# An encoder layer in float32: seven block products instead of eight for one request's MLP, and a pass of its own for the other's

## The chip, the cores and the metric

The kernel runs on one core of a Trainium2 chip. The metric is the device time of one execution in microseconds. Three executions of the kernel before took 2460.19 to 2464.03 us, with a median of 2462.54 us.

## The reference, cut to what matters

One layer of a bidirectional encoder runs on two requests with shared weights: the prompt (512 tokens of 1024 numbers) and the sample (1024 tokens). The change touches the last step, the MLP with a squared ReLU, with 4096 hidden columns.

```python
D_MODEL = 1024
BATCH = 1
SEQ = 512
...
DEC_BATCH = 1
DEC_SEQ = 1024
...
D_FF = 4 * D_MODEL
...
def squared_relu_mlp(x, w_up, w_down):
    return jnp.square(jax.nn.relu(x @ w_up)) @ w_down

def encoder_trunk(x, mem, ln_in_g, ln_in_b, w_in, rpb, g_mix_a, g_mix_b, w_out, ln1_g, ln1_b,
                  w_xq, w_xkv, w_xo, ln2_g, ln2_b, w_up, w_down, ln3_g, ln3_b):
    x = layer_norm(x, ln_in_g, ln_in_b)
    for l in range(DEPTH):
        x = layer_norm(ALPHA * x + token_mixer(x, w_in[l], rpb[l], g_mix_a[l], g_mix_b[l], w_out[l]),
                       ln1_g[l], ln1_b[l])
        x = layer_norm(ALPHA * x + memory_cross_attention(x, mem, w_xq[l], w_xkv[l], w_xo[l]),
                       ln2_g[l], ln2_b[l])
        x = layer_norm(ALPHA * x + squared_relu_mlp(x, w_up[l], w_down[l]), ln3_g[l], ln3_b[l])
    return x
...
def reference(x_prompt, x_sample, mem_prompt, mem_sample, ln_in_g, ln_in_b, w_in, rpb, g_mix_a,
              g_mix_b, w_out, ln1_g, ln1_b, w_xq, w_xkv, w_xo, ln2_g, ln2_b, w_up, w_down,
              ln3_g, ln3_b):
    y_prompt = encoder_trunk(x_prompt, mem_prompt, ln_in_g, ln_in_b, w_in, rpb, g_mix_a, g_mix_b,
                             w_out, ln1_g, ln1_b, w_xq, w_xkv, w_xo, ln2_g, ln2_b, w_up, w_down,
                             ln3_g, ln3_b)
    y_sample = encoder_trunk(x_sample, mem_sample, ln_in_g, ln_in_b, w_in, rpb, g_mix_a, g_mix_b,
                             w_out, ln1_g, ln1_b, w_xq, w_xkv, w_xo, ln2_g, ln2_b, w_up, w_down,
                             ln3_g, ln3_b)
    return (y_prompt, y_sample)
```

## The kernel before

All matrix products are made in three passes to keep float32's accuracy. An operand x is split into a high part (a copy rounded to float32r by ScalarE) and a low part (x minus the high part, by GpSimd or VectorE). `mm3` then sums high*high, high*low and low*high in PSUM, so 128 x 128 stationary and 128 x 512 moving columns cost three matmuls (L127 to L129).

The tokens lie in three groups of 512: group 0 is the prompt, groups 1 and 2 are the halves of the sample. Phase 0 makes the memory's keys and values, phase 1 the two attention mixtures, phase 2 the output projection, the cross-attention and the second layer norm. `ln2` (from L803) normalises a tile of 128 tokens, transposes it on TensorE and splits the result into high and low parts (L137 and L138); `X2[g]` holds the two parts of the transposed group.

Phase 3, from L851, is the MLP. The outer loop (L900) runs over 32 blocks f of 128 hidden columns. Per f, `col_block` loads 128 columns of `w_up` in two pieces of 256 KB, and `down_weights` loads 128 rows of `w_down` in two more; a piece goes through one of two `wraw` buffers, is copied by ScalarE (L104, L882) and subtracted by GpSimd (L105, L883). The buffer is free again when GpSimd is done. For each of the three groups, `up` makes 24 matmuls into a bank `pj`, then ScalarE applies the ReLU (L871), VectorE squares (L872), ScalarE copies the high part (L874) and GpSimd makes the low part (L875). `down` makes 24 matmuls, three to a bank of `t` or `s` for each of four token tiles and two halves of the columns, and VectorE adds every bank to the sums in `toks` (L897). So one pair of weight blocks serves 144 matmuls: 72 up and 72 down.

The last three blocks are handled apart (`LAST`, from L906): their hidden columns are kept, so that one tile of tokens after the other is finished, normalised by `layer_norm` (L147 on) and stored while TensorE still works on the next.

What stands in program order is not what runs in order: a scheduler of the framework orders each engine's instructions ahead of time by its own estimate. At run time each engine takes its list strictly in that order, and the DMAs all stand in one list, SyncE's. SBUF is cut into fixed slots: `tok` 8, `qt`, `pt`, `gb`, `kv` 2 each of 1024 columns, `cpr` 2 and `q` 7 of 512 and 528, six big `act` tiles, and in `wp` three `wh`, three `wl` and the two `wraw`.

## Time and profile before

| | us |
|---|---|
| median of three executions | 2462.54 |
| lowest and highest | 2460.19, 2464.03 |
| the profiled execution, from the first to the last instruction (span) | 2464.6 |
| TensorE busy in it | 2391.0 |
| VectorE, ScalarE, GpSimd busy | 1468.6, 858.5, 867.0 |

The profiled execution's own time is known by its span; it lies 2.1 us, or 0.1%, above the median. Busy times are sums over all stages. TensorE's matmuls overlap in the pipeline (one takes 390 ns from start to end while the next starts far earlier), so the number of matmuls that start in a stretch says more than the time of one.

### The profile page before, as it was taken

The numbers are of one execution on the slowest core, as the hardware profiler recorded it, in microseconds if no ns is written. First come the engines' busy times: TensorE is split into PE (matmuls) and PEld (weight loads), VectorE is DVE, ScalarE is ACT, GpSimd is POOL, SyncE is SP. The second block draws the span as 40 slices with busy tenths as digits, with TensorE's granted clock in tenths as the row PEclk, the third lists the DMA queues.
The fourth block names the chain that finished last, engine by engine and source line by source line (L and its number), as shares of the span: only waits on it lengthen the run. The fifth ranks groups of instructions, "written<-read, shape, count | busy, mean of one in ns | idle before, by whom it ended". The sixth has DMA issues, their size and how long they took to land.

```text
span 2464.6 us, 32262 instructions
## 1 busy us (share of the span) xinstructions
PE 2391.0 (97%) x11512; PEld 1983.0 (80%) x11512; DVE 1468.6 (60%) x3054; ACT 858.5 (35%) x1887; POOL 867.0 (35%) x790
## 2 busy tenths in 40 slices
PE   8989999999999999999999999999999999999997
PEld 6868778888888778778778788888888888888886
DVE  6256546666666785666666755555555555555538
ACT  4346645555555534333233211111111111111122
POOL 7555442221243135332353332222222223323346
PEclk9999999999999999999999999999999999999999
DMA  9665345554344543335323301111101011111112
GB/s 322 200 191 163 83 126 136 125 119 108 75 117 121 162 132 121 120 121 169 103 94 117 106 26 34 35 35 35 33 28 35 26 35 35 30 31 35 35 35 103
DMA packets 254641, 231.45 MB, mean 94 GB/s; under 512 B 65680, under 2 KB 196752, under 8 KB 254480
## 3 DMA queue, kind: packets, MB, share of 16 engines
q1 hardware_dynamic: 254480, 229.39, 32.2%
q8 instruction: 91, 1.49, 0.3%
q14 instruction: 70, 0.57, 0.1%
HBM read 170.16 MB, written 34.10 MB: 83 GB/s over the span
## 4 chain that ended last, share of the span: by engine, by line
PE 80%; DVE 6%; DMA 2%; ACT 2%; issue 1%; POOL 1%; SPq 0%; DVEq 0%; POOLq 0%; ACTq 0%
PE pj L127 15%; PE pj L128 15%; PE pj L129 15%; PE s L127 4%; PE s L129 4%; PE s L128 4%; PE t L127 3%; PE t L128 3%; PE t L129 3%; PE o L489 3%; PE t L473 2%; PE s L447 2%; PE s L448 1%; DVE tok L158 1%; PE t L499 1%
## 5 line engine op out<-in xcount | busy, mean ns | idle before, releaser
L105 POOL TENSOR_TENSOR wl<-wraw,wh 128x512 fp32r<-128x512 f32 x144 | 192.5, 1354 | 371.1 <-ACT wh L104 304.3
L897 DVE TENSOR_TENSOR tok<-tok,s 128x512 f32<-128x512 f32 x232 | 158.3, 685 | 234.5 <-PE s L129 234.3
L104 ACT ACTIVATE wh<-wraw 128x512 fp32r<-128x512 f32 x144 | 84.7, 625 | 305.5 <-PE pj L128 197.5
L431 ACT ACTIVATE q<-q,st 128x256 f32<-128x256 f32 (+3 forms) x256 | 138.3, 545 | 75.3 <-DVE st L430 72.5
L897 DVE TENSOR_TENSOR tok<-tok,t 128x512 f32<-128x512 f32 x232 | 152.0, 683 | 9.8 <-PE t L129 9.2
L477 DVE TENSOR_TENSOR pt<-t,pt 128x512 fp32r<-128x512 f32 x160 | 105.4, 671 | 85.6 <-ACT pt L476 85.1
L883 POOL TENSOR_TENSOR wl<-wraw,wh 128x512 fp32r<-128x512 f32 x64 | 84.0, 1330 | 185.3 <-ACT wh L882 180.9
L295 POOL TENSOR_TENSOR wl<-wraw,wh 128x256 fp32r<-128x256 f32 x128 | 94.4, 761 | 150.8 <-ACT wh L294 137.1
L871 ACT ACTIVATE cpr<-pj 128x512 f32<-128x512 f32 x96 | 56.9, 592 | 253.2 <-PE pj L129 251.7
L872 DVE TENSOR_TENSOR cpr<-cpr 128x512 f32<-128x512 f32 x96 | 93.1, 970 | 78.9 <-ACT cpr L871 78.8
L875 POOL TENSOR_TENSOR qt<-cpr,qt 128x512 fp32r<-128x512 f32 x45 | 61.5, 1366 | 190.1 <-ACT qt L874 146.5
L476 ACT ACTIVATE pt<-t 128x512 fp32r<-128x512 f32 x160 | 89.5, 583 | 88.5 <-PE o L489 85.0
L875 POOL TENSOR_TENSOR pt<-cpr,pt 128x512 fp32r<-128x512 f32 x46 | 64.7, 1407 | 156.6 <-ACT pt L874 149.3
L489 PE MATMUL o<-pt,tok 128*128 128x256 f32 (+3 forms) x560 | 113.5, 313 | 5.7 <-ACT q L495 4.1
L117 POOL TENSOR_TENSOR wl<-wraw,wh 128x512 fp32r<-128x512 f32 x48 | 63.2, 1333 | 126.1 <-ACT wh L116 120.6
L127 PE MATMUL pj<-x20h,wh 128*128 128x512 f32 x256 | 100.0, 391 | 0.1
L127 PE MATMUL pj<-x22h,wh 128*128 128x512 f32 x256 | 99.9, 390 | 0.0
L127 PE MATMUL pj<-x21h,wh 128*128 128x512 f32 x256 | 99.8, 390 | 0.0
L128 PE MATMUL pj<-x20l,wh 128*128 128x512 f32 x256 | 99.8, 390 | 0.0
L128 PE MATMUL pj<-x21l,wh 128*128 128x512 f32 x256 | 99.8, 390 | 0.0
L129 PE MATMUL pj<-x21h,wl 128*128 128x512 f32 x256 | 99.8, 390 | 0.0
L128 PE MATMUL pj<-x22l,wh 128*128 128x512 f32 x256 | 99.8, 390 | 0.0
(381 smaller groups left out, 7216.9 us busy)
## 6 DMA issues: line engine op xcount, KB each, us to landing
wraw<-in_w_in_dram SPq DMA_DIRECT2D x96, 256.0 KB
wraw<-in_w_up_dram SPq DMA_DIRECT2D x64, 256.0 KB
wraw<-in_w_down_dram SPq DMA_DIRECT2D x64, 256.0 KB
kv<-in_c_rope_dram SPq DMA_DIRECT2D x24, 512.0 KB
hd<-qt SPq DMA_DIRECT2D x96, 128.0 KB
wraw<-in_w_out_dram SPq DMA_DIRECT2D x48, 256.0 KB
wraw<-in_w_xq_dram SPq DMA_DIRECT2D x48, 256.0 KB
wraw<-in_w_xo_dram SPq DMA_DIRECT2D x48, 256.0 KB
```

The source lines that it names most:

```text
L105: G.tensor_sub(wl[:, sl], r, f32(wh[:, sl]))
L127: T.matmul(out, lh[k], rh[k], start=(k == 0), stop=False, skip_group_check=True)
L128: T.matmul(out, lh[k], rl[k], start=False, stop=False, skip_group_check=True)
L129: T.matmul(out, ll[k], rh[k], start=False, stop=(k == n - 1), skip_group_check=True)
L295: G.tensor_sub(dl, src, f32(dh))
L431: A.activation(p, p, AF.Exp, bias=nm, accum_out=den)
L476: A.activation(hi[:, 0:x], t[:, 0:x], AF.Copy)
L477: V.tensor_sub(lo[:, 0:x], t[:, 0:x], f32(hi[:, 0:x]))
L489: T.matmul(o[:, q0:q0 + n], v(c, h), part[:, x:x + n], start=(done == 0 and part is hi), stop=(done == total - 1 and part is lo), skip_gro ...
L872: V.tensor_mul(a, a, a)
L875: G.tensor_sub(hl, a, f32(hh))
L897: V.tensor_add(x, x, q)
```

## The change

The sample's 1024 tokens are no longer run as two groups with eight block products per projection. Each of its two MLP matrix products is seen as a product of 2 x 2 blocks: the left operand (tokens, or hidden columns) in two halves of the rows and two of the inner dimension, the weights likewise. Seven block products are formed from sums and differences of blocks and combined into the four output blocks by additions. `PRODUCTS` lists for each of the seven which left blocks and which weight blocks are added or subtracted, and into which output blocks the result goes, with its sign; five of the seven need a sum on the left, five a sum of weights, and five go into two output blocks, two into one.

- `ln2` keeps the sample's transposed tokens in float32 (one tile per half; no split), and writes all normalised tokens to DRAM (`x2s`).
- The prompt's MLP is a loop of its own: per f the same four weight pieces now serve 24 up and 24 down matmuls. The hidden low part is made by VectorE.
- In its rounds 3 to 9, `left` forms the seven left operands of the sample's up projection: VectorE adds (five of seven), ScalarE copies the high part, VectorE makes the low part in a `kv` slot, and a DMA of 512 KB stores it in DRAM (`sa`): 28 tiles.
- The sample's up projection: for each of the seven products the left operand is loaded again (2 MB), and for each of 16 blocks f one or two weight pieces of 256 KB are loaded into `q` slots, added by VectorE if two, copied by ScalarE and subtracted by GpSimd (`right`); 12 matmuls follow into one bank, and the bank is copied (ScalarE) or added (VectorE) to the hidden columns, which stay in SBUF in float32. A finished hidden block is squared by VectorE.
- The sample's down projection: for each product 16 steps c. VectorE forms the left sum (five of seven products), ScalarE and VectorE split it, VectorE forms the weight sum (five of seven) and its low part; 12 matmuls go into four banks that hold the sums of all 16 steps. Then the four banks are added to one or two blocks of the output. GpSimd has no part in this.
- `finish` normalises and stores a half of the sample: the first half behind the sixth product, so beside the seventh, the second half at the very end.

The core of the diff:

```diff
-    x2s = dr.tile([512, D], F32, name="x2s")
+    x2s = dr.tile([1536, D], F32, name="x2s")
+    sa = [dr.tile([4, P, 2, 512], F32, name=f"sa{i}") for i in range(7)]
...
-            X2.append(new_act(f"x2{gi}"))
+            X2.append(new_act("x20") if gi == 0 else act.tile([P, 8, 512], F32, name=f"xt{gi}", tag="act"))
             GB[gi] = [[bcast(d[n][0], "gb")] for n in ("ln2_g", "ln2_b")]
-        layer_norm(toks[gi][t], *GB[gi])
+        x = toks[gi][t]
+        layer_norm(x, *GB[gi])
+        S.dma_start(x2s[(4 * gi + t) * P:(4 * gi + t + 1) * P], x)
         if gi == 0:
-            S.dma_start(x2s[t * P:(t + 1) * P], toks[gi][t])
-        split_t(toks[gi][t], *X2[gi], t * P)
+            split_t(x, *X2[0], t * P)
+            return
+        for kk in range(2):
+            o = bank("t").rearrange("p (j c) -> p j c", j=4)
+            for j in range(4):
+                T.transpose(o[:, j, :], x[:, (4 * kk + j) * P:(4 * kk + j + 1) * P], ident)
+            A.activation(X2[gi][:, 4 * kk:4 * kk + 4, t * P:(t + 1) * P], o, AF.Copy)
...
+    PRODUCTS = {
+        1: (((0, 0), ADD, (1, 1)), ((0, 0), ADD, (1, 1)), (((0, 0), ADD), ((1, 1), ADD))),
+        2: (((1, 0), ADD, (1, 1)), ((0, 0),), (((1, 0), ADD), ((1, 1), SUB))),
...
+    UP, DOWN = (5, 3, 2, 4, 1, 7, 6), (3, 5, 4, 2, 7, 1, 6)
...
+    def left(i):
+        blk = lambda b, k: X2[1 + b[0]][:, 4 * b[1] + k]
+        what = PRODUCTS[i][0]
+        for k in range(4):
+            x = blk(what[0], k)
+            if len(what) > 1:
+                y = slot("cpr")
+                V.tensor_tensor(y, x, blk(what[2], k), op=what[1])
+                x = y
+            t = slot("kv", dt=F32R)
+            A.activation(t[:, 0:512], x, AF.Copy)
+            V.tensor_sub(t[:, 512:1024], x, f32(t[:, 0:512]))
+            S.dma_start(sa[i - 1][k], f32(t).rearrange("p (j c) -> p j c", j=2))
...
-    toks[0] = [slot(tag) for tag in ("kv", "kv", "gb", "gb")]
+    toks[0] = [slot("tok") for _ in range(4)]
...
-        hh, hl = dst or parts(("pt", "qt")[next(turn) % 2])
+        hh, hl = slot("q", 512, F32R), slot("q", 512, F32R)
...
-        G.tensor_sub(hl, a, f32(hh))
+        V.tensor_sub(hl, a, f32(hh))
...
-    LAST = 3
-    for f in range(32 - LAST):
+    def down(h, w, first):
+        for t in range(4):
+            tt = slice(t * P, (t + 1) * P)
...
+    for f in range(32):
         w, dn = col_block(wup, f * P), down_weights(f)
-        for g in range(3):
-            h = up(g, w)
+        down(up(w), dn, f == 0)
+        if 3 <= f < 10:
+            left(UP[f - 3])
+    gb3 = [[bcast(d[n][0], "gb")] for n in ("ln3_g", "ln3_b")]
+    for t in range(4):
+        layer_norm(toks[0][t], *gb3, 1)
+        S.dma_start(outs[0][0, t * P:(t + 1) * P], toks[0][t])
...
+    def hidden(b, f):
+        if b not in H:
+            H[b] = ([slot("tok") for _ in range(8)] if b == (1, 0) else
+                    [act.tile([P, 8, 512], F32, name=f"h{b[0]}{b[1]}", tag="act") for _ in range(2)])
+        if b == (1, 0):
+            return H[b][f // 2][:, f % 2 * 512:f % 2 * 512 + 512]
+        return H[b][f // 8][:, f % 8]
...
+    def square(b, f):
+        x = hidden(b, f)
+        V.scalar_tensor_tensor(x, x, 0.0, x, op0=ALU.max, op1=ALU.mult)
...
+    def right(what, load, low, tag=None):
...
+        x = load(what[0])
+        if len(what) > 1:
+            z = load(what[2])
+            y = slot("cpr")
+            V.tensor_tensor(y, x, z, op=what[1])
+            x = y
+        t = wp.tile([P, 1024], F32R, name="wh", tag=tag or ("wh", "wl")[next(ring) % 2])
+        A.activation(t[:, 0:512], x, AF.Copy)
+        low.tensor_sub(t[:, 512:1024], x, f32(t[:, 0:512]))
+        return t[:, 0:512], t[:, 512:1024]
...
+    done = set()
+    lefts = {0: left_load(0), 1: left_load(1)}
+    for n, i in enumerate(UP):
+        _, what, into = PRODUCTS[i]
+        xs_ = lefts.pop(n)
+        for f in range(16):
+            if f == 8 and 0 < n < 6:
+                lefts[n + 1] = left_load(n + 1)
+            wh_, wl_ = (x.rearrange("p (k c) -> p k c", k=4) for x in right(what, up_block(f), G))
+            o = bank(("pj", "s", "t")[f % 3])
+            mm3(o, [wh_[:, k] for k in range(4)], [wl_[:, k] for k in range(4)],
+                [xs_[k][:, 0] for k in range(4)], [xs_[k][:, 1] for k in range(4)])
+            for b, op in into:
+                h = hidden(b, f)
+                if (b, f) not in done:
+                    done.add((b, f))
+                    A.activation(h, o, AF.Copy, scale=1.0 if op == ADD else -1.0)
+                else:
+                    V.tensor_tensor(h, h, o, op=op)
+            b = {2: (0, 1), 7: (1, 0), 6: (0, 0)}.get(i)
+            if b is not None:
+                square(b, f)
...
+    def finish(h):
+        for t in range(4):
+            layer_norm(accs[h][t], [g3[:, 0], g3[:, 1]], [g3[:, 2], g3[:, 3]], 1 if t % 2 else 2)
+            row = 512 * h + t * P
+            S.dma_start(outs[1][0, row:row + P], accs[h][t])
...
+    for n, i in enumerate(DOWN):
+        lw, rw, into = PRODUCTS[i]
+        banks = [bank(tag) for tag in (("pj", "pj", "s", "s") if n % 2 == 0 else ("t", "t", "t", "o"))]
+        for c in range(16):
+            x = hidden(lw[0], c)
+            if len(lw) > 1:
+                y = wp.tile([P, 512], F32, name="wraw", tag="wraw", bufs=2)
+                V.tensor_tensor(y, x, hidden(lw[2], c), op=lw[1])
+                x = y
+            a = wp.tile([P, 1024], F32R, name="wh", tag="wh")
+            A.activation(a[:, 0:512], x, AF.Copy)
+            V.tensor_sub(a[:, 512:1024], x, f32(a[:, 0:512]))
+            rh, rl = right(rw, down_block(c), V, "wl")
             for t in range(4):
-                down(g, t, [h], [dn], first=(f == 0))
-    # the last blocks' hidden columns are kept, so that a tile of tokens is finished at once
-    hs = [[None] * LAST for _ in range(3)]
-    ws = [col_block(wup, f * P) for f in range(32 - LAST, 32)]
-    for g in range(3):
-        hs[g][0] = up(g, ws[0])
-    hs[0][1] = up(0, ws[1])
-    hs[0][2] = up(0, ws[2], (slot("q", 512, F32R), slot("q", 512, F32R)))
-    keep = [act.tile([P, 8, 512], F32R, name="keep", tag="act") for _ in range(2)]
-    for i in (1, 2):
-        for g in (1, 2):
-            n = 4 * (i - 1) + 2 * (g - 1)
-            hs[g][i] = up(g, ws[i], (keep[0][:, n], keep[1][:, n]))
-    dn = [down_weights(f) for f in range(32 - LAST, 32)]
-    for g in range(3):
+                lh, ll = a[:, t * P:(t + 1) * P], a[:, 512 + t * P:512 + (t + 1) * P]
+                T.matmul(banks[t], lh, rh, start=(c == 0), stop=False)
+                T.matmul(banks[t], lh, rl, start=False, stop=False)
+                T.matmul(banks[t], ll, rh, start=False, stop=(c == 15))
+            if n == 0:
+                square((1, 1), c)
         for t in range(4):
-            down(g, t, hs[g], dn)
-            layer_norm(toks[g][t], g3, b3, 2 if g == 2 and t >= 2 else 1)
-            n = 4 * g + t
-            dst = outs[0][0, n * P:(n + 1) * P] if g == 0 else outs[1][0, (n - 4) * P:(n - 3) * P]
-            S.dma_start(dst, toks[g][t])
+            for b, op in into:
+                x = accs[b[0]][t][:, b[1] * 512:(b[1] + 1) * 512]
+                if (b, t) not in done:
+                    done.add((b, t))
+                    V.scalar_tensor_tensor(x, x, ALPHA, banks[t], op0=ALU.mult, op1=op)
+                else:
+                    V.tensor_tensor(x, x, banks[t], op=op)
+        if i == 7:
+            g3 = act.tile([P, 8, 512], F32, name="g3", tag="act")
+            for j, name in enumerate(("ln3_g", "ln3_b")):
+                src = d[name][0]
+                S.dma_start(g3[:, 2 * j:2 * j + 2].rearrange("p a c -> p (a c)"),
+                            bass.AP(tensor=src.tensor, offset=src.offset, ap=[[0, P], [1, D]]))
+        if i == 1:
+            finish(0)
+    finish(1)
```

Three places in the engines' lists. The first is SyncE's list in the MLP. Before, a round of the loop is four weight pieces and nothing else (`wraw` is the buffer, the source is the weight):

```order
L90 DMA wraw_17253<-in_w_down_dram 128x512
L90 DMA wraw_17472<-in_w_up_dram 128x4x128
L90 DMA wraw_17476<-in_w_up_dram 128x4x128
L90 DMA wraw_17482<-in_w_down_dram 128x512
L90 DMA wraw_17486<-in_w_down_dram 128x512
```

With the change, in the prompt's rounds 3 to 9 (L91 is the weight load, L888 the store of a left operand's tile from a `kv` slot):

```order
L91 DMA wraw_14586<-in_w_up_dram 128x4x128
L888 DMA sa2_66<-kv_14452 128x1024
L91 DMA wraw_14592<-in_w_down_dram 128x512
L888 DMA sa2_66<-kv_14456 128x1024
L91 DMA wraw_14596<-in_w_down_dram 128x512
L888 DMA sa2_66<-kv_14460 128x1024
L888 DMA sa1_65<-kv_14558 128x1024
L91 DMA wraw_14690<-in_w_up_dram 128x4x128
```

Stores that wait for VectorE now stand between the weight pieces, and the pieces behind a store wait with it.

The second is VectorE's list. Before, in a round of the MLP (L897 adds a PSUM bank to the sums, L872 is the square):

```order
L897 TENSOR_TENSOR tok_9425<-tok_9425,t_14806 128x512
L897 TENSOR_TENSOR tok_11153<-tok_11153,s_14669 128x512
L897 TENSOR_TENSOR tok_9457<-tok_9457,t_14816 128x512
L897 TENSOR_TENSOR kv_13959<-kv_13959,s_14730 128x512
L872 TENSOR_TENSOR cpr_14861<-cpr_14861 128x512
L897 TENSOR_TENSOR tok_9489<-tok_9489,t_14826 128x512
L897 TENSOR_TENSOR kv_13960<-kv_13960,s_14740 128x512
L897 TENSOR_TENSOR gb_13961<-gb_13961,s_14750 128x512
L897 TENSOR_TENSOR gb_13962<-gb_13962,s_14760 128x512
```

With the change, in the sample's down projection, in the fifth of the seven products in `DOWN` order, which has sums on both sides (L1037 the left sum, L960 the weight sum, L1041 and L964 their low parts):

```order
L1037 TENSOR_TENSOR wraw_21410<-h01_17138,h11_17467 128x512
L960 TENSOR_TENSOR cpr_21419<-q_21415,q_21417 128x512
L1037 TENSOR_TENSOR wraw_21436<-h01_17138,h11_17467 128x512
L960 TENSOR_TENSOR cpr_21445<-q_21441,q_21443 128x512
L1041 TENSOR_TENSOR wh_21412<-wraw_21410,wh_21412 128x512
L964 TENSOR_TENSOR wh_21421<-cpr_21419,wh_21421 128x512
L1041 TENSOR_TENSOR wh_21438<-wraw_21436,wh_21438 128x512
L1037 TENSOR_TENSOR wraw_21462<-h01_17138,h11_17467 128x512
L964 TENSOR_TENSOR wh_21447<-cpr_21445,wh_21447 128x512
L960 TENSOR_TENSOR cpr_21471<-q_21467,q_21469 128x512
```

Per step c four instructions that read two operands from SBUF stand where before mostly additions from PSUM stood.

The third is VectorE's list behind the end of the sixth product, with the rows of L960 and L1037 left out; L1057 adds the banks to the output's blocks, and L151 to L153 belong to `finish(0)`.

```order
L1057 TENSOR_TENSOR gb_19755<-gb_19755,t_21730 128x512
L1057 TENSOR_TENSOR pt_19752<-pt_19752,t_21731 128x512
L1057 TENSOR_TENSOR kv_19756<-kv_19756,t_21731 128x512
L1057 TENSOR_TENSOR pt_19753<-pt_19753,o_21732 128x512
L1057 TENSOR_TENSOR kv_19757<-kv_19757,o_21732 128x512
L151 BN_STATS lnst_22157<-qt_19750 128x6
L152 BN_STATS lnst_22169<-qt_19751 128x6
L1041 TENSOR_TENSOR wh_22265<-wraw_22263,wh_22265 128x512
L964 TENSOR_TENSOR wh_22274<-cpr_22272,wh_22274 128x512
L151 BN_STATS lnst_22169<-qt_19751 128x6
L1041 TENSOR_TENSOR wh_22291<-wraw_22289,wh_22291 128x512
L964 TENSOR_TENSOR wh_22300<-cpr_22298,wh_22300 128x512
```

The layer norm of the first half of the sample stands between the low parts (L1041, L964) that the seventh product's matmuls wait for.

## Rows read from the trace of the kernel before

**Rows 1.** The page: parts 1 and 2, busy time and 40 slices in tenths.

```profile
PE 2391.0 (97%) x11512; PEld 1983.0 (80%) x11512; DVE 1468.6 (60%) x3054; ACT 858.5 (35%) x1887; POOL 867.0 (35%) x790
PE   8989999999999999999999999999999999999997
DVE  6256546666666785666666755555555555555538
```

**Rows 2.** Busy time by stretch: length, engines with instructions, clock, DMA share, GB/s.

```profile
1000.00:1400.00 400.00, 380.50 (x1849) 312.92 (x1848) 264.67 (x465) 140.66 (x291) 147.84 (x112) 0.98 0.38 120
1400.00:1600.00 200.00, 198.88 (x878) 163.00 (x877) 111.40 (x168) 38.71 (x65) 54.55 (x42) 1.00 0.12 35
1600.00:2200.00 600.00, 600.00 (x2618) 491.45 (x2617) 333.78 (x488) 106.40 (x183) 168.81 (x128) 1.00 0.11 32
20.00:40.00 20.00, 16.95 (x79) 13.78 (x77) 17.12 (x23) 10.75 (x18) 19.25 (x12) 1.00 1.05 339
```

**Rows 3.** The timeline of VectorE in one steady round: start us, us, instruction.

```profile
1599.80 0.68 DVE L897 TENSOR_TENSOR kv<-kv,t 128x512 f32<-128x512 f32 x1
1600.40 0.68 DVE L897 TENSOR_TENSOR gb<-gb,t 128x512 f32<-128x512 f32 x1
...
1611.59 1.67 DVE L872 TENSOR_TENSOR cpr<-cpr 128x512 f32<-128x512 f32 x1
...
1630.24 0.69 DVE L872 TENSOR_TENSOR cpr<-cpr 128x512 f32<-128x512 f32 x1 [3.41 <-ACT cpr L871]
1630.85 1.28 DVE L897 TENSOR_TENSOR tok<-tok,s 128x512 f32<-128x512 f32 x2
```

**Rows 4.** The same round on GpSimd.

```profile
1610.16 2.55 POOL L105 TENSOR_TENSOR wl<-wraw,wh 128x512 fp32r<-128x512 f32 x2 [9.53 <-ACT wh L104]
```

**Rows 5.** The line L872 alone: duration in ns, least, median, most.

```profile
L872 DVE TENSOR_TENSOR cpr<-cpr x96: 682/693/1670, 1394.6 to 2400.6; 128x512 f32<-128x512 f32 x96
```

**Rows 6.** The page, part 5: three groups of the weight path and of evacuation.

```profile
L104 ACT ACTIVATE wh<-wraw 128x512 fp32r<-128x512 f32 x144 | 84.7, 625 | 305.5 <-PE pj L128 197.5
L883 POOL TENSOR_TENSOR wl<-wraw,wh 128x512 fp32r<-128x512 f32 x64 | 84.0, 1330 | 185.3 <-ACT wh L882 180.9
L871 ACT ACTIVATE cpr<-pj 128x512 f32<-128x512 f32 x96 | 56.9, 592 | 253.2 <-PE pj L129 251.7
```

**Rows 7.** The timeline of the DMA queue's issues while phase 2 streams weights.

```profile
963.46 1.61 SPq L90 DMA_DIRECT2D wraw<-in_w_xq_dram  x2
968.91 1.58 SPq L90 DMA_DIRECT2D wraw<-in_w_xo_dram  x2
...
973.81 1.69 SPq L90 DMA_DIRECT2D wraw<-in_w_xo_dram  x2
979.83 1.63 SPq L90 DMA_DIRECT2D wraw<-in_w_xq_dram  x2
...
989.18 0.39 SPq L90 DMA_DIRECT2D wraw<-in_w_xq_dram  x1
...
998.81 2.28 SPq L90 DMA_DIRECT2D wraw<-in_w_xo_dram  x2
```

**Rows 8.** The timeline of TensorE at the end.

```profile
2448.56 0.39 PE L129 MATMUL s<-wh,keep 128*128 128x512 f32 x1
```

**Rows 9.** The chain that ended last, in order of time, its last 12 us.

```profile
2450.37 1.14 issue
...
2452.25 0.60 DVE lnst L150
...
2457.25 0.46 issue
...
2458.57 0.53 issue
...
2460.44 0.60 DVEq L986
```

**Rows 10.** The same chain earlier: two halves of a layer norm's first step.

```profile
2447.88 1.32 DVE tok L158 x2
```

67 lines of the change are left out of this document (47 added, 20 removed).

## The prediction

> **What bounds the kernel now.** I read the page's first two parts first. TensorE is busy for 97% of the span, VectorE for 60%, and in the last 40% of the span VectorE is mostly at half load [rows 1]. An average can hide stages, so busy time by stretch came next. In the MLP's steady state TensorE has not one microsecond of idle time in 600, and 2618 matmuls start in it, one per 0.229 us, at a granted clock of 1.00, the upper of its two levels (2.4 GHz); in phase 2, by contrast, it idles for 5% and the clock is granted at 0.98 [rows 2]. The end: the last matmul starts at 2448.56 and is over at 2448.95 [rows 8], so 15.65 us of the span of 2464.6 lie behind it and belong to VectorE's layer norm and the last store. So the MLP is bound by TensorE up to its last matmul, and a matmul less is worth 0.229 us, as long as whatever feeds TensorE keeps up. The rest of the working asks that of every feeder.
>
> Two facts on the feeders. VectorE's instructions on 128 x 512 take 0.68 to 0.69 us, yet in a row the next starts 0.60 to 0.61 us after the last [rows 3], so 0.61 us is the price of one. An instruction with two operands in SBUF also waits while GpSimd runs one of its own: the square at 1611.59 took 1.67 us, since GpSimd was at work from 1610.16 to 1612.71 [rows 3, 4]; undisturbed it takes 0.69 [rows 5]. Additions with an operand in PSUM are not held up.
>
> **The matmuls.** The sample's two projections need 2 x 1536 matmuls before and 2 x 7 x 16 x 12 = 2688 after; the prompt's 1536 stay. That is 384 fewer, at 0.229 us 88.0 us. Against the profiled span: 2464.6 - 88.0 = 2376.6 us, if TensorE stays as dense as it is. Now what can keep it from that.
>
> **The prompt's own pass: 25 us (0 to 55).** Before, four weight pieces served 144 matmuls, 33 us. Now they serve 48, 11.0 us, so two pieces every 5.50 us. There are two buffers for the raw pieces, and a buffer goes through load, ScalarE's copy (0.63 us) and GpSimd's subtraction (1.33) [rows 6] before the next load may be issued. Phase 2 shows this cycle running freely: loads in pairs are issued at 963.46, 968.91, 973.81 and 979.83, every 5.45, 4.90 and 6.02 us, 5.46 on average [rows 7]. So a cover that did not matter before is now used up to its last tenth. With only a round and a half of blocks in hand, late cycles are not all made up by early ones; I take 5.7 us, between the mean and the longest: 64 cycles x 0.2 = 13 us. Bounds: 0, and 64 x 0.52 = 33 us at 6.02.
> In the rounds in which the left operands are made it is worse. VectorE's own work per round is 10 instructions (8 additions, the square, the low part), 6.1 us. To it come 48 instructions (20 sums, 28 low parts), which the list spreads over some eight rounds: 3.7 us each. GpSimd's four subtractions keep it busy for 5.3 of 11 us, so each of the 8 instructions per round with two SBUF operands meets it with a chance of 0.48 and waits 0.65 us on average, 2.5 us in all. That is 12.3 us against 11.0, and 8 x 1.3 is 10 to 12 us; I take 12. The stores of the left operands wait for VectorE in SyncE's list, and the weight pieces stand behind them, so the two delays feed each other. Bounds: 0 if they hide in the free rounds, 22 if most of 48 x 0.61 = 29 us shows. Together 25.
>
> **The sample's up projection: 5 us (0 to 43).** A block takes TensorE 12 x 0.229 = 2.75 us. ScalarE has at most 1.8 us of work in that time [rows 6] (a copy of weights and two of banks). The loads are at most two pieces of 256 KB per block and 2 MB of left operand per product, 655 KB per 2.75 us or 238 GB/s; at the start of the kernel the queues moved 339 GB/s [rows 2], and seven buffers hold three and a half blocks. So VectorE and GpSimd decide. In the fourth product VectorE has a weight sum, two additions and a square, 2.44 us; in products 2, 6 and 7 three instructions, 1.83, and so in the fifth. If GpSimd's 1.33 us held VectorE up wholly, these would be 3.77 and 3.16 us, and the loss 16 x 1.02 + 64 x 0.41 = 43 us. But the additions come from PSUM and run under GpSimd's work, six weight slots and seven banks let either side be late, and half the squares in rows 5 met no delay at all. I take 5. Nothing can be gained: TensorE does the same per matmul.
>
> **The sample's down projection: 2 + 13 us (5 to 39).** 2.75 us per step again, with GpSimd out of it. VectorE has three instructions per step in four products, 1.8 us, and four in the three products with both sums, 2.44 us. At the seams between products 4 or 8 additions come in a row, up to 4.9 us; two prepared steps are 5.5 us of matmuls. I take 2 us for all six seams, at most 15. The seventh product is another matter: 64 instructions x 0.61 = 39 us, 8 additions of the sixth product 4.9, and the layer norm of the first half, 8 statistics at 0.60 [rows 9], eight halves of the first step at 0.66 [rows 10], four more halves and small ones, 13.3 us. That is 57 us against 44 of matmuls. A lead of two or three steps takes some away, GpSimd's additions of the layer norm (1.3 us each) put as much back: 13 us, between 5 and 24.
>
> **The end: 5 us (3 to 10).** Before, most tiles were finished under matmuls. Now four tiles are normalised behind the last one: 12 additions and statistics x 0.60, ten half steps x 0.66, 0.7 of small ones, less 1.2 us that can run before the last matmul: 13.3 us. Waits for GpSimd of 1.14, 0.46 and 0.53 us were in the last chain [rows 9]; I add 3.5 of these. From VectorE's end at 2461.04 to the span's end it was 3.6 us [rows 9]. Sum 20.4 against 15.65.
> Phase 2 loses 16 subtractions of VectorE (the sample's tokens are no longer split there) and gains eight stores. TensorE idled just 1.1 of the 200 us around its end [rows 2], so at most 1 us is won.
>
> Sum: 2376.6 + 25 + 5 + 2 + 13 + 5 = 2426.6 us. The profiled execution lies 2.1 us above the median, so 2424.5, or **2425 us**. With all lower bounds it is 2381, with all upper ones 2521.
>
> **A rule beside it.** Rows 3 say that VectorE's next instruction starts 0.08 us before the last has ended. The Trainium skill, "VectorE: DVE Perf Modes", section Terms, says that the pipeline is drained after every operation and the next cannot issue until it is empty. By that rule an instruction in a row costs its 0.69 us, and the sum would be 16 us higher; the trace, with 0.60 us from start to start, speaks against it, for additions with an operand in PSUM.
>
> **The rivals.**
> Everything stays covered. For it: TensorE showed no idle time through 600 us with a VectorE at 56%, and the mean of the three cycles is 5.46 against 5.50. Then only the layer norm's lower end (5) and the end (3) are left: 2376.6 + 8 - 2.1 = 2383 us, to 2400 with small losses.
> VectorE is slower in long rows of two-SBUF instructions. Rows 3 show such a row for PSUM operands only; two such instructions in a row are not shown. At 0.69 instead of 0.61 a step with both sums takes 2.76 us, as long as its matmuls, and there is no time left for the seams: about 74 instructions per product x 0.08 = 6 us in two products, all of it late by 3 to 5 us, and 94 x 0.08 = 8 in the seventh, 16 us in all: 2441 us.
> Slower than before, by the two raw buffers in the prompt's pass. If the two later pairs of rows 7 (989.18, 998.81) count as well, the mean cycle is 35.35 / 5 = 7.07 us. Those waited for a full set of weight blocks, so they are no free cycle; but stores in the same list and a ScalarE that waits in order could bring them about here. 64 x (7.07 - 5.50) = 100 us instead of 25: 2424.5 + 75 = 2500 us. It decides from a cycle of 6.48 us: 62.9 us over 64 cycles is what the matmuls leave after the other 25.
> That the change doesn't cut the matmuls is excluded by the lists: 384 fewer stand there.
>
> **How the numbers follow.** My forecast, partial losses of 25 to 75 us, has 0.55; everything covered 0.20; the slower VectorE 0.10; the weight cycle 0.13; something in between, near the old time, 0.02. The range leaves out the weight cycle and little more at either end: 2384 to 2456 us. About 0.2%, 5 us, is what a measurement here can tell from no change: faster than 2457.6 has 0.83 (a little of the first case lies higher, a little of the last lower), within 5 us 0.05, slower 0.12.
>
> **What would show it.** Right: the spacing of matmuls stays at 0.229 us where they are dense; TensorE shows its idle time in the rounds with left operands and beside the first half's layer norm; 20 us lie behind the last matmul; weight loads of the prompt's pass are issued as soon as GpSimd is done. Wrong: rounds of the prompt's pass of 13 us and more (the cycle), idle time in all of the up projection (GpSimd against VectorE), or a down projection in which the products with both sums take over 46 us and the others 44.

## The result and the profile after

The changed kernel takes 2431.20 us (median of four executions, 2430.11 to 2432.93) against 2462.54; the ratio is 0.9875, 95% interval 0.9861 to 0.9889. The forecast was 2425 us, the range 2384 to 2456. The profiled execution's span is 2431.2 us.

The page after, parts 1 and 2 (compare [rows 1]): TensorE has 384 matmuls less, and is now busy for 95% instead of 97%; VectorE went from 60% to 69%.

```profile
PE 2321.2 (95%) x11128; PEld 1916.6 (79%) x11128; DVE 1667.1 (69%) x3294; ACT 1034.1 (43%) x2181; POOL 910.0 (37%) x798
PE   8989999999999999999989989999999999999995
DVE  6266545666656776658576679666655799887997
```

Both kernels start the first matmul on the prompt's transposed tokens (`x20`) at 1387.2 us of the span, so in these two executions all of the difference lies behind it. Busy time by stretch (columns as in [rows 2]), first of before from there to its last matmul, then of after: the whole, the rounds behind the first four, the last three products of the up projection, six products of the down projection, and the seventh.

```profile
1387.00:2449.00 1062.00, 1060.75 (x4641) 868.47 (x4640) 603.31 (x898) 199.72 (x341) 329.68 (x248) 1.00 0.12 36
```

```profile
1387.00:2412.00 1025.00, 989.04 (x4257) 801.44 (x4256) 803.72 (x1141) 375.56 (x634) 372.71 (x255) 0.99 0.54 171
1440.00:1740.00 300.00, 286.88 (x1209) 228.83 (x1208) 211.03 (x298) 106.23 (x179) 138.31 (x101) 0.98 0.44 144
1950.00:2086.00 136.00, 131.47 (x560) 106.71 (x559) 131.35 (x149) 30.15 (x48) 65.20 (x44) 0.97 0.74 225
2086.00:2348.00 262.00, 261.61 (x1153) 215.93 (x1152) 226.19 (x366) 111.48 (x191) 0.00 (x0) 1.00 0.53 172
2349.00:2412.00 63.00, 48.30 (x191) 36.95 (x189) 53.45 (x93) 20.84 (x34) 20.61 (x8) 0.95 0.33 114
```

Before, 4640 matmuls start in 1061.4 us, 0.2287 us each, and TensorE idles for a microsecond. After, 4256 start in 1024.4 us, where the same pace would take 973.4: 51.0 us are lost, and the end is 3.6 us longer (19.6 us from the start of the last matmul against 16.0). Cut at the starts of the block products' first matmuls:

| part | forecast, us | measured, us |
|---|---|---|
| prompt's pass and first block product, 1760 matmuls in 425.9 us | 25 | 23.4 |
| up projection, products 2 to 7, 1152 matmuls in 273.1 us | 5 | 9.6 |
| down projection, products 1 to 6, 1152 in 262.2 us | 2 | -1.3 |
| the seventh, 192 in 63.2 us | 13 | 19.3 |
| behind the last matmul | 5 | 3.6 |
| sum, against 2376.6 us | 50 | 54.6 |

Part of these losses lies in TensorE's clock. Before, every matmul of this stretch ran at a granted clock of 1.00. After, TensorE fell to 0.50, the lower of its two levels (1.2 GHz), six times between the pass's first matmul and the last, each time in or just behind a gap in which two matmuls started 1.6 to 5.8 us apart, since TensorE waited. At that level a matmul starts every 0.43 us. Three of the stretches, in the prompt's pass, at the start of the up projection's seventh product and in the seventh of the down projection:

```profile
1456.30:1461.30 5.00, 4.92 (x12) 3.85 (x13) 5.00 (x9) 1.30 (x3) 2.76 (x2) 0.50 0.91 308
2039.10:2045.00 5.90, 5.90 (x14) 4.66 (x15) 5.83 (x7) 1.20 (x2) 3.32 (x2) 0.50 0.61 178
2365.90:2369.30 3.40, 3.40 (x9) 2.64 (x8) 3.40 (x3) 0.00 (x0) 2.72 (x2) 0.50 0.00 0
```

55 matmuls ran so and took 11.2 of the 51.0 us more than at 0.2287: 5.1 in the first part, 2.9 in the up projection, 3.2 in the seventh product. Most of the rest is time in which TensorE had nothing to start. So these waits cost more than their own length.

### The profile page after: what moved, and what is told of

The parts are those of the page before. It is cut to its first block, busy times and chain, and to the rows that moved or that the text cites. A ratio compares the mean times of both kernels' runs of the same rounds, so it can differ in the third digit from the quotient of the medians.

```text
span 2431.2 us, 33241 instructions
## 1 busy us (share of the span) xinstructions
PE 2321.2 (95%) x11128; PEld 1916.6 (79%) x11128; DVE 1667.1 (69%) x3294; ACT 1034.1 (43%) x2181; POOL 910.0 (37%) x798
## 4 chain that ended last, share of the span: by engine, by line
PE 38%; DVE 9%; DMA 4%; issue 3%; POOL 2%; ACT 1%; POOLq 0%; SPq 0%; DVEq 0%; ACTq 0%
PE pj L128 5%; PE pj L129 5%; PE pj L130 5%; DVE cpr L960 2%; PE s L128 2%; PE s L130 2%; PE s L129 2%; PE t L128 2%; PE t L130 2%; PE t L129 2%; PE t L1045 1%; PE t L1046 1%; PE t L1047 1%; DVE h L1001 1%; DMA q<-in_w_up_dram 1%
## 5 line engine op out<-in xcount | busy, mean ns | idle before, releaser
L960 DVE TENSOR_TENSOR cpr<-q 128x512 f32<-128x512 f32 x160 | 148.8, 931 | 47.4 <-DMA q<-in_w_up_dram 19.2
L963 ACT ACTIVATE wh<-cpr 128x512 fp32r<-128x512 f32 x160 | 100.3, 627 | 161.5 <-DVE cpr L960 140.2
L105 ACT ACTIVATE wh<-wraw 128x512 fp32r<-128x512 f32 x144 | 87.9, 629 | 182.3 <-DMA wraw<-in_w_up_dram 50.3
L964 POOL TENSOR_TENSOR wh<-cpr,wh 128x512 fp32r<-128x512 f32 x80 | 114.4, 1431 | 115.7 <-ACT wh L963 115.7
L925 DVE TENSOR_TENSOR tok<-tok,s 128x512 f32<-128x512 f32 x124 | 83.5, 681 | 41.1 <-PE s L130 41.0
L925 DVE TENSOR_TENSOR tok<-tok,t 128x512 f32<-128x512 f32 x124 | 83.1, 682 | 31.7 <-PE t L130 31.6
L130 PE MATMUL pj<-x20h,wl 128*128 128x512 f32 x256 | 102.1, 399 | 2.2 <-POOL wl L106 2.1
L1040 ACT ACTIVATE wh<-wraw 128x512 fp32r<-128x512 f32 x80 | 50.6, 633 | 119.0 <-issue 40.8
L474 PE MATMUL t<-ident,q 128*128 128x128 f32 x624 | 94.9, 274 | 2.2 <-DVE pt L478 1.0
L490 PEld LDWEIGHTS o<-pt,tok 128*128 128x128 f32 x560 | 83.5, 192 | 11.3 <-ACT q L496 6.2
L428 DVE CUSTOM_DVE_ANT_0 q<-s,gb 128x256 f32<-128x256 f32 (+2 forms) x160 | 67.9, 466 | 27.4 <-PE s L449 21.6
```

The costliest lines, as they stand in the source:

```text
L130: T.matmul(out, ll[k], rh[k], start=False, stop=(k == n - 1), skip_group_check=True)
L490: T.matmul(o[:, q0:q0 + n], v(c, h), part[:, x:x + n], start=(done == 0 and part is hi), stop=(done == total - 1 and part is lo), skip_gro ...
L925: V.tensor_add(x, x, q)
L960: V.tensor_tensor(y, x, z, op=what[1])
L963: A.activation(t[:, 0:512], x, AF.Copy)
L964: low.tensor_sub(t[:, 512:1024], x, f32(t[:, 0:512]))
```

## The experiments

The profiled executions reach the prompt's pass at 1383.0 to 1392.7 us, though the work ahead of it is the same in all of them. So small effects are read from the stretch behind that point, from the pass's first matmul to the last of all (1024.4 us in the changed kernel), and from the parts that an edit touches. Each comes from one profiled execution. Where an edit leaves a part alone, it still varies: the prompt's pass with the first block product took 424.8 to 429.3 us, products 2 to 7 of the up projection 271.8 to 273.3, the seventh product of the down projection 63.2 to 65.1. All edits are to the changed kernel; ratios are to the kernel before.

### The prompt's pass

One left operand in place of seven:

```diff
-        if 3 <= f < 10:
-            left(UP[f - 3])
+        if f == 3:
+            left(UP[0])
...
-            S.dma_start(f32(t[k]), sa[UP[n] - 1][k])
+            S.dma_start(f32(t[k]), sa[UP[0] - 1][k])
```

> Leaves out six of the seven left operands: only product 5's is made, in round 3, and all seven products of the up projection load that one (so the numbers of the sample are wrong, the work after it is the same). My theory: the prompt's rounds 3 to 11 are 13.7 us long on average instead of 11.0 because the left operands are made in them, 9 x 2.7 = 24 us. Six sevenths of that go: 2431 - 21 = 2410 us, and the rounds after the fifth come down to 11.0. Rival (the weight cycle of the two raw buffers is slow by itself in this part of the pass, or the first rounds of the pass are slow for want of prepared blocks): the rounds stay at 13 us and the time within 4 us of 2431.

Measured: 2419.18 us, ratio 0.9822 (0.9805 to 0.9839), stretch 1011.0, 13.3 us less. Rounds 7 on (numbered from 0) take 11.1 us on average, those before still up to 16. So the left operands cost, but less than the 21 us expected here; a gap of 6.5 us remained at 1451 us of the span. In the changed kernel it stands there too, and its SyncE list shows why (start us, us, instruction; L91 are weight pieces, L888 stores of a left operand, L980 its reloads for the up projection):

```profile
1434.88 0.38 SPq L91 DMA_DIRECT2D wraw<-in_w_up_dram  x1
1436.26 0.33 SPq L980 DMA_DIRECT2D qt<-sa  x1
1437.18 0.38 SPq L91 DMA_DIRECT2D wraw<-in_w_up_dram  x1
1437.73 1.66 SPq L888 DMA_DIRECT2D sa<-kv  x2
1443.23 0.32 SPq L980 DMA_DIRECT2D qt<-sa  x1
1444.51 0.32 SPq L980 DMA_DIRECT2D pt<-sa  x1
1445.23 0.81 SPq L91 DMA_DIRECT2D wraw<-in_w_down_dram  x2
...
1452.94 0.38 SPq L91 DMA_DIRECT2D wraw<-in_w_up_dram  x1
```

The scheduler put the first operand's reloads, needed 300 us later, right behind its stores. SyncE waits there until the stores have landed, and nothing is issued from 1439.4 to 1443.2; the down weights, behind it, are copied by ScalarE at 1450.94 (in the next kernel at 1445.19), the up weights after them, and TensorE waits 5.4 us for that. Waits of SyncE and of TensorE around it, by what ended them (us in total, times, longest):

```profile
SPq L980 <- DMA sa<-kv: 5.6, 3, 3.8
...
PE pj L128 <- ACT wh L105: 5.4, 1, 5.4
```

That operand written straight into the slots that the up projection reads:

```diff
-            t = slot("kv", dt=F32R)
+            t = slot(("qt", "qt", "pt", "pt")[k] if i == UP[0] else "kv", dt=F32R)
...
+            if i == UP[0]:
+                first.append(t.rearrange("p (j c) -> p j c", j=2))
+                continue
...
-    lefts = {0: left_load(0), 1: left_load(1)}
+    lefts = {0: first, 1: left_load(1)}
```

> Product 5's left operand is written straight into the four slots in which the up projection reads it; its four stores and four reloads are gone, all else is as in the changed kernel. Theory (TensorE's 5.6 us gap at 1450 us of the span, which was there too with six operands left out, 6.5 us, comes from reloads that stand in SyncE's list and wait there for the stores of the same tiles, 3.8 us at the longest, with two weight loads behind them): that gap goes, and the stretch from the pass's first matmul to the last falls from 1024.4 to 1018 or 1019 us. Rival (the gap is VectorE's load in that round): it stays at over 4 us, the stretch within 2 us.

Measured: 2424.13 us (0.9840, 0.9826 to 0.9855), stretch 1017.3, 7.1 less; TensorE's longest gap around that place is 1.6 us. The theory holds, but the gain isn't the 5.4 us of the wait alone: other gaps grew by some 2 us, and 7 instead of 25 matmuls of the pass ran at half clock, 3.6 us less.

Six operands made, but not stored:

```diff
-            S.dma_start(sa[i - 1][k], f32(t).rearrange("p (j c) -> p j c", j=2))
+            if i == UP[0]:
+                S.dma_start(sa[i - 1][k], f32(t).rearrange("p (j c) -> p j c", j=2))
...
-            S.dma_start(f32(t[k]), sa[UP[n] - 1][k])
+            S.dma_start(f32(t[k]), sa[UP[0] - 1][k])
```

> All seven left operands are made as in the changed kernel, but only the first is stored, and all products load that one (the sample's numbers are wrong). Tells VectorE's load from the stores in SyncE's list. Theory that VectorE's 48 extra instructions set the rounds: within 4 us of the changed kernel's 2431. Rival, that the weight pieces wait in SyncE's list behind stores that wait for VectorE: as with the left operands left out, 2410 us. If both count, between: 2415 to 2425.

Measured: 2435.61 us (0.9887, 0.9873 to 0.9902), stretch 1026.4: no gain. The other operands' stores are not what costs (the gap of the first operand's reload is still there). One tile per round, then (`left(i, k)` makes a single tile):

```diff
-        if 3 <= f < 10:
-            left(UP[f - 3])
+        if 2 <= f < 30:
+            left(UP[(f - 2) // 4], (f - 2) % 4)
```

> The same 28 left-operand tiles, made one per round in rounds 2 to 29 of the prompt's pass instead of four per round in rounds 3 to 9; nothing left out. Theory (VectorE's load per round decides): 48 instructions over 28 rounds add 1.05 us to each, about 9.7 of 11.0 us, so the rounds fit; the stretch from the pass's first matmul to the kernel's last (1024.4 us in the changed kernel, 1011.0 with six operands left out) comes down to 1009 to 1013 us, the time to 2419. Rival (each store in SyncE's list holds up weight loads wherever it stands): the loss is spread too, the stretch stays above 1020 us.

Measured: 2427.67 us (0.9851, 0.9833 to 0.9870), stretch 1021.8, 2.6 less. The 12 us didn't come; the loss had spread, in some 15 gaps, most of 0.4 to 1.2 us, half of them for weights, half for VectorE's additions. The long gap of the reload is gone here too (the longest is 2.3 us), so this edit and the direct operand partly bring the same gain. My theory was short of something, and its two candidates went into the next two kernels: raw buffers of their own for the up weights, without and with the spreading.

```diff
-        w, dn = col_block(wup, f * P), down_weights(f)
+        w, dn = col_block(wup, f * P, "gb" if f > 3 else None), down_weights(f)
```

> In the prompt's pass the up weights of rounds 4 to 31 are loaded raw, 512 KB at once, into the two gb slots that are free there, so that the two raw buffers serve the down weights alone and their cycle may take 11 us; the left operands stay in rounds 3 to 9. Theory A (the rounds with left operands are bound by VectorE's work): the stretch from the pass's first matmul to the last stays within 4 us of the changed kernel's 1024.4 us, the 5.6 us gap of the reload aside. Theory B (they are bound by the cycle of the raw buffers, held up through SyncE's and ScalarE's lists): 1010 to 1014 us, rounds of 11 us from the fifth on.

> One left-operand tile per round, as in the spread version (which brought 2.6 us of the 12 expected: TensorE had a gap of 0.5 to 1.2 us in most rounds, eight of 15 for a low part or a copy of up weights), and the up weights with raw buffers of their own. Theory B (with VectorE's work spread, what was left is the raw buffers' cycle): the gaps of rounds 5 on go, the stretch is 1009 to 1013 us. Theory A' (GpSimd against VectorE, or the stores): it stays at 1018 us or more.

Measured: alone 2429.45 us (0.9869, 0.9854 to 0.9884), stretch 1023.6, 0.8 less, with the pass inside what unchanged passes take; with the spreading 2416.01 us (0.9818, 0.9801 to 0.9835), stretch 1007.1, 17.3 less. The stretch 1440 to 1740 us of the spread version, of own buffers, and of both (the changed kernel's row is above):

```profile
1440.00:1740.00 300.00, 290.23 (x1230) 230.05 (x1230) 217.84 (x299) 107.19 (x182) 141.78 (x104) 0.99 0.43 141
```

```profile
1440.00:1740.00 300.00, 285.68 (x1217) 227.91 (x1216) 206.99 (x299) 99.84 (x176) 145.76 (x103) 0.99 0.44 143
```

```profile
1440.00:1740.00 300.00, 298.20 (x1287) 240.84 (x1286) 218.56 (x314) 105.51 (x188) 161.50 (x108) 1.00 0.46 148
```

1209 matmuls became 1230 and 1217 with one edit each, and 1287 with both. So there are two limits of about the same height, the burst of left operands and the cycle of the raw buffers: to take one away shows the other. That is why each edit alone looked like a refutation. The reload's long gap is gone in all three, so the 17.3 us contain that gain as well. What in the burst is the limit isn't separated: spreading it thins VectorE's work, ScalarE's copies and the stores in SyncE's list at once.

### The up projection

```diff
-            wh_, wl_ = (x.rearrange("p (k c) -> p k c", k=4) for x in right(what, up_block(f), G))
+            wh_, wl_ = (x.rearrange("p (k c) -> p k c", k=4) for x in right(what, up_block(f), V))
```

> In the sample's up projection the low parts of the weight blocks are made by VectorE instead of GpSimd; nothing else. Theory (VectorE's two-SBUF instructions wait while GpSimd runs its own, which makes products 4 to 7 in order take 45.1 to 47.0 us instead of 43.6): GpSimd then does nothing there, VectorE has at most four instructions per block, 4 x 0.61 = 2.44 of 2.75 us, and the products come down to 43.6 to 44.2 us: 2431 - 9 = 2422 us. Rival 1 (VectorE takes 0.69 us per instruction in such rows, 2.76 per block, so it becomes the bound): the three products with four instructions take 46 to 47 us as before, the others 43.6, within 3 us of 2431. Rival 2 (the loads of weights and left operands are late): no change either, and TensorE's gaps end with a DMA.

Measured: 2424.21 us (0.9842, 0.9827 to 0.9857), stretch 1016.4, 8.0 less; the products take 43.6 to 44.4 us, and TensorE has no gap in them. One block at the turn from the sixth to the seventh product on VectorE (L960 weight sum, L1001 addition from PSUM, L950 square) and on GpSimd (low parts) of the changed kernel:

```profile
2041.26 0.67 DVE L1001 TENSOR_TENSOR h<-h,s 128x512 f32<-128x512 f32 x1
2041.96 0.69 DVE L950 SCALAR_TENSOR_TENSOR h<-h 128x512 f32<-128x512 f32 x1
2042.57 1.77 DVE L960 TENSOR_TENSOR cpr<-q 128x512 f32<-128x512 f32 x1
```

```profile
2042.14 1.66 POOL L964 TENSOR_TENSOR wh<-cpr,wh 128x512 fp32r<-128x512 f32 x1 [1.35 <-ACT wh L963]
2045.14 1.68 POOL L964 TENSOR_TENSOR wh<-cpr,wh 128x512 fp32r<-128x512 f32 x1 [1.35 <-ACT wh L963]
```

The sum, 0.69 us alone, takes 1.77 since it is held until GpSimd ends at 2043.80; GpSimd's next subtraction needs that sum, through ScalarE's copy, and in it meets the square (1.66 us instead of 1.33 [rows 6]). So the two run in lockstep: a block comes every 3.0 us (2042.14 to 2045.14) where its matmuls take 2.75 at full clock. While TensorE was in the fourth product, and VectorE had a square, a sum and two additions per block, a block came every 3.25 us; in most of the fifth, with a sum and two additions but no square, every 2.65, so three instructions alone don't hold it up. TensorE lives on prepared blocks for a while and then waits, 1.8 and 1.6 us around the start of the fifth product and 3.7 us ahead of the seventh, and starts the seventh at half clock (the second of the rows on the clock, with the result). The additions from PSUM beside it stay at 0.67 us. The Trainium skill, "SBUF — State Buffer", section "SBUF: two separate sides", describes this as a lock on a shared pair of ports, held for a whole instruction by GpSimd or by a VectorE instruction with two SBUF operands; these rows agree. With the low part on VectorE, four instructions in a row, each with two SBUF operands but the first, start 0.60 us apart, 2.75 us per block:

```profile
2029.73 0.69 DVE L1001 TENSOR_TENSOR h<-h,pj 128x512 f32<-128x512 f32 x1 [0.23 <-PE pj L130]
2030.34 0.69 DVE L960 TENSOR_TENSOR cpr<-q 128x512 f32<-128x512 f32 x1
2030.94 0.69 DVE L964 TENSOR_TENSOR wh<-cpr,wh 128x512 fp32r<-128x512 f32 x1
2031.54 0.69 DVE L950 SCALAR_TENSOR_TENSOR h<-h 128x512 f32<-128x512 f32 x1
2032.48 0.69 DVE L1001 TENSOR_TENSOR h<-h,pj 128x512 f32<-128x512 f32 x1 [0.26 <-PE pj L130]
```

### The seventh product and the end

The stores of the first half issued by GpSimd:

```diff
-            S.dma_start(outs[1][0, row:row + P], accs[h][t])
+            (S if h else G).dma_start(outs[1][0, row:row + P], accs[h][t])
```

> The four stores of the sample's first half are issued by GpSimd, which is otherwise idle there, instead of standing in SyncE's list among the weight loads of the seventh product. Theory (of the seventh product's 19.6 us too many, the 4.4 us gap at 2396 us of the span, during which VectorE idles for 5.1 us, is the fourth store waiting in SyncE's list for its layer norm, with loads behind it): that gap goes, the seventh takes 57 to 59 us instead of 63.2. Rival (all of it is VectorE's load): within 1.5 us of 63.2.

Measured: 2425.58 us (0.9845, 0.9831 to 0.9860), stretch 1017.5, 6.9 less; the seventh takes 57.2 us and the gap is gone. In the changed kernel three lists hang together there. VectorE:

```profile
2392.49 0.68 DVE L1037 TENSOR_TENSOR wraw<-tok,h 128x512 f32<-128x512 f32 x1
2398.24 0.69 DVE L960 TENSOR_TENSOR cpr<-q 128x512 f32<-128x512 f32 x1 [5.07 <-issue]
```

GpSimd (the last additions of the first half's layer norm, and the same of the second half at the end), and SyncE (L1028 stores, L1017 weights, and its wait for GpSimd: us, times, longest):

```profile
2382.26 12.06 POOL L170 TENSOR_TENSOR pt<-pt,g 128x512 f32<-128x512 f32 x2 [0.83 <-ACT pt L166]
...
2424.54 3.02 POOL L170 TENSOR_TENSOR kv<-kv,g 128x512 f32<-128x512 f32 x2 [0.83 <-ACT kv L166]
```

```profile
2371.58 9.54 SPq L1017 DMA_DIRECT2D q<-in_w_down_dram  x8
2383.57 11.11 SPq L1028 DMA_DIRECT2D out_dram<-pt  x2
2394.78 2.61 SPq L1017 DMA_DIRECT2D q<-in_w_down_dram  x5
...
SPq L1028 <- POOL pt L170: 10.3, 1, 10.3
```

Two additions that take 3.0 us at the end of the kernel take 12.1 here, for VectorE runs one two-SBUF instruction after the other and leaves GpSimd no opening. The store waits for GpSimd, the weights stand behind the store, and VectorE runs out of weights at 2393.17. Then GpSimd ends, at 2394.32, and the weights go out. TensorE, idle until 2400.19, runs its next matmuls at half clock:

```profile
2400.20:2403.40 3.20, 3.20 (x8) 2.52 (x9) 3.20 (x6) 1.26 (x2) 0.00 (x0) 0.50 0.19 74
```

With the stores on GpSimd the same two additions took longer still, but no weights stood behind them:

```profile
2383.17 19.89 POOL L170 TENSOR_TENSOR pt<-pt,g 128x512 f32<-128x512 f32 x2 [0.83 <-ACT pt L166]
```

The other part of the loss, by moving the layer norm to a product with less work on VectorE:

```diff
-    UP, DOWN = (5, 3, 2, 4, 1, 7, 6), (3, 5, 4, 2, 7, 1, 6)
+    UP, DOWN = (5, 3, 2, 4, 1, 7, 6), (3, 5, 4, 7, 1, 2, 6)
...
+            if i == 2 and c % 4 == 3:
+                finish(0, [c // 4])
...
-        if i == 1:
-            finish(0)
```

> The down projection's products run in the order 3, 5, 4, 7, 1, 2, 6, so that the first half of the sample is complete after five products, and its four layer norms stand one by one behind the 4th, 8th, 12th and 16th step of product 2, which has three VectorE instructions per step (29 us of 44) instead of four. Theory (the seventh product's 63.2 us instead of 43.5 are VectorE's overflow by the layer norm): the seventh comes down to 44 to 46 us, product 2 to 44 to 47, 2431 - 17 = 2414 us. Rival (layer norm hurts wherever it stands, by GpSimd's additions and the load of its constants): product 2 takes 55 to 60 us and the time is within 5 us of 2431. Rival (the seventh is slow by itself, since both sums are in it): it stays above 55 us.

Measured: 2428.06 us (0.9847, 0.9826 to 0.9867), stretch 1020.7. The seventh takes 44.5 us, so it isn't slow by itself; but product 2 takes 55.0 instead of the 47 at most that I had allowed, and the time is within 5 us of 2431: the signs of the first rival. Together they take 99.4 us against 106.7 for the last two in the old order: of some 19 us too many, 12 moved along with the norm.

The last three steps token tile by token tile:

```diff
+            late.append((c, a, rh, rl))
+            if n == 6 and 13 <= c < 15:
+                continue
             for t in range(4):
...
+                for cc, a_, rh, rl in late:
```

> In the seventh product of the down projection the last three steps run token tile by token tile: nine matmuls each into the first bank, then the second, so the four banks of the second half are complete about 2.06 us apart instead of all in the last 0.7 us. Theory (19.2 us behind the last matmul are four layer norms in a row on VectorE and GpSimd, about 3.3 us each): the first norms run under the last 18 matmuls, and 13 to 15 us remain behind the last matmul; the seventh product gets longer by 0 to 3 us, since three prepared steps must be in hand. Total gain 2 to 6 us: 2425 to 2429. Rival (the end is set by waits between ScalarE, GpSimd and the stores, not by the row of norms): over 18 us remain.

Measured: 2431.42 us (0.9874, 0.9858 to 0.9890), 19.6 us from the start of the last matmul as before. The scheduler undid the edit: in the trace the last matmuls still alternate between the four banks, and the first bank's addition starts 0.9 us ahead of the last matmul. So the run says nothing on the theory, which stays open.

### All together

Spreading, own raw buffers, the direct operand, VectorE's low parts in the up projection and the stores by GpSimd:

> All that helped at once: left operands spread over rounds 2 to 29, raw buffers of their own for the up weights, product 5's left operand written straight into its slots, the up projection's low parts by VectorE, the first half's stores issued by GpSimd. If the gains add (7.9 for VectorE's low parts, 6.8 for the stores, 7.0 for the reload, 2.6 for spreading, 0 to 8 for the raw buffers): a stretch of 992 to 1000 us against 1024.4 and a time of 2399 to 2407 us. If reload and raw buffers are one and the same gain, or the gains share a cause: 2408 to 2414 us.

Measured: 2397.39 us (0.9746, 0.9732 to 0.9760), stretch 988.0, both a little below the ranges. By the cuts of the table above: 2.5 us lost in the pass, 0.3 and -1.3 in the next two parts, 13.2 in the seventh product, where 9.1 us of TensorE's waits end with VectorE's low parts (L968, in this kernel, is that of the weights); eight matmuls ran at half clock, all of them there:

```profile
PE pj L1050 <- DVE wh L968: 9.1, 5, 3.1
```

Then the layer norm moved as above and made wholly by VectorE:

> The combination before (988.0 us from the pass's first matmul to the last), with the down projection's products in the order 3, 5, 4, 7, 1, 2, 6, the first half's layer norms behind every fourth step of product 2, and these norms wholly on VectorE, without GpSimd. The last two products hold 112 instructions of steps, 16 additions and four norms of about 4.0 us on VectorE: 128 x 0.60 + 16 = 93 us against 87.1 of matmuls, where the combination before takes 43.5 + 57.1 = 100.6. Theory (VectorE's work, and its waits for GpSimd, set the last two products): 92 to 95 us, a stretch of 980 to 983 and a time of 2390 to 2393 us. Rival (the layer norm costs more by its place in the lists than by its work): over 98 us, no gain.

Measured: 2395.80 us (0.9742, 0.9725 to 0.9759), stretch 983.5; the last two products take 96.2 us instead of 100.6, 1 us over the theory's range. The two times can't be told apart, the stretches can. All four norms run within the first 35 us of product 2, where VectorE is without a pause, and in the last product it idles for 5 us, nearly all at its end; so a part of what is left may lie in the order of VectorE's list, which no run here tests. This run also moves the norm and takes GpSimd out of it in one step, so their shares aren't known. Both kernels beat the changed one by 34 to 35 us.

## Why the prediction was right, point by point

**The matmuls.** 384 fewer at the old pace: right. Four of the down projection's products even take 43.5 us for 192, 0.2267 us each, a little less than the 0.2287 before; why, no run here tells.

**The prompt's pass**, 25 forecast, 23.4 measured, but not by the shares that I gave. Of the 13 us for the weight cycle in all rounds nothing is seen where no left operand is made: the later rounds take 11.0 us. The 12 us for the left operands were too few, and part of them was a cause that I had missed, the reloads in SyncE's list (7.1 us by the direct operand). I had written that VectorE's and SyncE's delays feed each other; the runs show that it is rather two limits side by side, the burst of left operands and the raw cycle, and that both must go (17.3 us) before either shows. The sum came out right with two wrong terms in it, and with 5.1 us at half clock that were in neither: that is luck.

**The up projection**, 5 of 0 to 43 forecast, 9.6 measured. The mechanism was right, as the kernel with low parts on VectorE shows. The size was off because I counted on chance meetings, with slots and banks to even them out; the sum, the copy and the low part form a loop, which settles into lockstep, at 3.25 us per block during the fourth product and 3.0 in the last two. 2.9 of the 9.6 us are the matmuls at half clock; but while they ran GpSimd caught up, so without them the seventh product would probably have lost time to the lockstep itself; no run here tells.

**The down projection.** The six products: 2 forecast, nothing lost. The seventh: 13 forecast, 19.3 measured. Without the stores among the weights some 13.2 us remain, which is close to the term as I had worked it out; the 6 us on top are the loop of GpSimd, store and weights, that was not in the working. That the 13.2 are VectorE's work is shown only in part: TensorE's waits there end mostly with VectorE's low parts, moving the norm moved most of the loss, and moving it with GpSimd taken out of it brought 4.4.

**The end**, 5 forecast, 3.6 measured, by two errors that nearly cancel. The chain that ended last, in order of time, shows two waits of 0.52 us between VectorE's steps, where I had added 3.5 us for such waits from [rows 9]. But from VectorE's end, at 2425.23, to the span's end it took 6.0 us instead of 3.6, since GpSimd's last additions run until 2427.56 and the store follows them:

```profile
2415.32 0.52 issue
...
2421.97 0.52 issue
...
2424.54 1.80 POOL kv L170
2426.34 1.22 POOLq L1127
```

VectorE's last instruction:

```profile
2424.54 0.69 DVE L168 TENSOR_TENSOR kv<-kv,g 128x512 f32<-128x512 f32 x1
```

**The clock.** The working kept TensorE at its upper level throughout. That the forecast still lies within 7 us of the time, though 11.2 us went to matmuls at half clock, is luck in part: the wait terms, taken as lengths of waits, were large enough to hold them.

**The rivals.** "VectorE is slower in rows of two-SBUF instructions" is refuted: they start 0.60 us apart, and the fifth and sixth products of the down projection, with both sums, took 44.0 and 43.5 us. By the rule in the Trainium skill, "VectorE: DVE Perf Modes", section Terms, it would have been 0.69; these rows speak against it for SBUF operands too. "Slower by the raw buffers" would have needed rounds of 13 us throughout; only rounds 3 to 11 were that long on average (13.7 us), and the cycle was one of several causes. "Everything covered", 2383 to 2400 us, is about where the combined version came to, so what it presumed was possible, but not in this order of work.

## What to carry to other kernels

When a long TensorE stage gives up matmuls, work out each feeder's load per round, and look for loops as well as loads: two engines that wait for each other's results settle at the loop's length, whatever the slack of each. Read the DMA list of the changed program for a transfer that must wait for something late (a reload of what was just stored, a store behind a layer norm): everything behind it is late too. Where TensorE may wait for some microseconds, look at the granted clock behind the wait and count the matmuls at half clock as well. And when taking away a suspected limit brings nothing, take the second one away as well before the first is acquitted.

## What the runs showed of the hardware

GpSimd can be kept waiting far longer than VectorE: two additions of 3.0 us took 12.1 and 19.9 us beside rows of VectorE instructions with two SBUF operands, whereas VectorE waited for a single GpSimd instruction at a time (its longest instruction of 128 x 512 behind the pass's start took 1.80 us here, and 2.90 in the combined version). After 4.3 us of idle time TensorE started eight matmuls 0.43 us apart at a granted clock of 0.50 (1.2 GHz), then one every 0.23 us at 1.00 (2.4 GHz) again. Not every gap did this: behind the 1.8 us ahead of the up projection's fifth product the granted clock stayed at 1.00.
